# Stationary tiles that begin at 64 modulo 128 bytes, in a two-layer decoder trunk on one core

## The chip, the cores and the metric

The kernel runs on one NeuronCore of a Trainium2 chip. The metric is the device time of one execution in microseconds (us); the kernel before has a median of 2036.69 us over 3 runs (2036.59 to 2038.44). The engines are named as the profile names them: PE is TensorE's matmul, PEld its loading of stationary operands, DVE is VectorE, ACT is ScalarE, POOL is GpSimd, SP is SyncE, which here issues the DMAs. Durations of one instruction are in nanoseconds (ns). A difference of 0.2% is about 4 us.

## What is computed

A batch of one sequence of 512 tokens, 1024 wide, goes through two layers. Each layer is a macaron: half-step SwiGLU feed-forward, token mixer, half-step SwiGLU feed-forward, each with a root-mean-square norm before and after.

```python
for layer in range(2):
    hf = silu(n @ w_gate) * (n @ w_up) @ w_down         # n = rms_norm(x), 1024 -> 2816 -> 1024
    x = x + 0.5 * rms_norm(hf)
    mix = attention(rms_norm(x)) if layer == 0 else mlstm(rms_norm(x))
    x = x + rms_norm(mix)
    x = x + 0.5 * rms_norm(second_swiglu(rms_norm(x)))
```

The attention of layer 0 has 8 stick-breaking heads and 8 dilated heads of 64 columns; the mLSTM of layer 1 has 8 heads of 128 columns. Input and output are float32.

## The kernel before

**Operands.** Every float32 operand of a large product is split into two tiles of the type float32r, `hi` (a rounded copy, made by ACT) and `lo` (the rest, made by DVE or POOL), 4 bytes an element each. A product is three matmuls, hi by hi, hi by lo and lo by hi (`mm3`), which PE adds up in PSUM. Each matmul has its own load of a 128x128 stationary tile, and then lets a moving tile of 128 to 512 columns pass; most have 512. In the profile a matmul's tiles read `out<-moving,stationary`: `pg<-xnh,whi` moves the activations `xnh` over the stationary weights `whi`.

**Stages.** Six phases follow each other: `f00`, `att`, `f01` (layer 0), `f10`, `mls`, `f11` (layer 1). A feed-forward phase (`ffn`) makes gate and up products, `pg<-xnh,whi`, 512 columns at a time, except for the first six chunks, which go by halves of 256 columns; the activation `h` (`glu`); and the down product, partly by a seven-product scheme (`products`, tiles `pc<-dhi,hhi`), partly directly (`po<-dhi,hhi`). There the down weights `dhi`, `dlo` move and the activations `hhi`, `hlo` are stationary. The mixers make projections (`pq`, `ob`), values (`pv<-whi,xnh`, 256 columns, where the weights move and the activations are stationary), heads (`z`, `pv<-p5hi,...`), and an output product (`po<-whi,mhi`, weights moving).

**Order.** The kernel writes the order of work out by itself: `tick` and `spawn` place the elementwise work between matmuls by a modelled clock that counts 0.417 ns a column, and `W` holds delays that were set in that clock. Weights come by DMA from SP through three `raw` buffers, are split by ACT and by DVE or POOL (`chunk`), and wait in four buffers each of `whi` and `wlo`.

**Where tiles lie.** Tiles come from pools, one after another along a partition. The helper `few` widens tiles of a few columns to 128 bytes. In the built program every matmul's moving tile and every stationary tile begins at a multiple of 128 bytes. PE loads the stationary tile of the next matmul while the moving tile of the current one passes, so two reads run side by side. The distance between these two starts (next stationary less current moving) is a multiple of 256 bytes for 6455 of the matmuls with 512 columns of float32r, and 128 more than a multiple for 524. Of these 524, the output products of the mixers (`po<-whi,mhi` and its two partners) are the largest part. With 256 columns it is a multiple of 256 for 1804, and 128 more for 431, the latter mostly in the first chunks of `f01` and `f11`.

Of the kernel before, what the change touches and what calls it, by code (L numbers as in the profile page):

```python
# [11 lines left out]
F32R = mybir.dt.float32r  # L12
# [4 lines left out]
P = 128  # L17
T = 512
D = 1024
KT = 8  # L20
TB = 4
# [21 lines left out]
class Trunk:  # L43
# [73 lines left out]
    def few(self, pool, n, name, bufs=1, dt=F32, rows=P):  # L117

        return pool.tile([rows, 32 if dt is F32 else 64], dt, tag=name, bufs=bufs, name=name)[:, :n]

    def bank(self, name):
        return self.ps.tile([P, 512], F32, tag="ps", name=name)

    def chunk(self, src, n=1024, pool=None, tag="w", bufs=4, eng=None):

        nc, pool = self.nc, pool or self.pp
        raw = self.pp.tile([P, 1024], F32, tag="raw", bufs=3, name="raw")
        nc.sync.dma_start(raw[:, :n], src)
        hi = pool.tile([P, 1024], F32R, tag=tag + "hi", bufs=bufs, name="whi")
        lo = pool.tile([P, 1024], F32R, tag=tag + "lo", bufs=bufs, name="wlo")  # L130
        nc.scalar.copy(hi[:, :n], raw[:, :n])  # L131
        sub = (eng or nc.vector).tensor_sub(lo[:, :n], raw[:, :n], hi[:, :n])  # L132
        if eng:
            self.tc.keep_in_program_order(sub)
        return hi, lo

    def gates(self, src):

        raw = self.pp.tile([P, 1024], F32, tag="raw", bufs=3, name="raw")
        self.nc.sync.dma_start(raw[:, :512], src)  # L140
        w = self.pp.tile([P, 1024], F32R, tag="whi", bufs=4, name="wg")
        v, s = w.rearrange("p (k s m) -> p k s m", k=KT, s=2), raw[:, :512].rearrange("p (k m) -> p k m", k=KT)
        self.nc.scalar.copy(v[:, :, 0, :], s)
        self.nc.vector.tensor_sub(v[:, :, 1, :], s, v[:, :, 0, :])
        return w
# [256 lines left out]

    def hop(self, src):

        hi, lo = [self.fp.tile([P, 256], F32R, tag=t, bufs=12, name=t) for t in ("hhi", "hlo")]
        self.split(hi, lo, src)
        return hi, lo

# [141 lines left out]
    def attention_heads(self, ap, mp, dp):  # L550
            nc, a = self.nc, self.a
            self.exp_ln()
            qk, vs, mix, gone = {}, {}, {}, set()
            done = {i: 0 for i in range(8)}
            cols = [(i, 4 + i) if i < 4 else (8 + i, 12 + i) for i in ORD]
            tri = ap.tile([P, 2, P], F32R, name="tri")
            trif = ap.tile([P, 2, P], F32, tag="f5", bufs=2, name="trif")
            nc.sync.dma_start(trif, a["tri"])
            nc.vector.tensor_copy(tri, trif)
            self.tri = tri  # L560
            self.spawn(self.toeplitz_rows(dp))
            cs = self.first()
            bs = [self.bank("pq") for _ in cs]
            for t in range(2):
                self.half(t)
                for b, c in zip(bs, cs):
                    self.proj(b, c, t * 256, t * 256 + 256)
            for i in range(2):
                self.later(W["qs"], qk, i, self.qk_split(*bs[2 * i:2 * i + 2]))
            scored = {i: 0 for i in range(8)}  # L570

            def lane(r):
                for n, i in enumerate(ORD):
                    while n not in qk:
                        yield 300
                    sl = slice(r * 64, r * 64 + 64)
                    core = self.stick(*qk[n], r) if i < 4 else self.dilated(*qk[n], r, 2 * (i - 4) + r)
                    wait = next(core)
                    scored[n] += 1
                    yield wait  # L580
                    hi, lo = yield from core
                    while i // 2 not in vs:
                        yield 300
                    pv = self.attend2(hi, lo, vs[i // 2][:, :, 2 * (i % 2) + r])
                    m = ap.tile([P, T], F32, tag="m", bufs=1, name="m")
                    nc.scalar.copy(m[sl, :], pv[64:, :])
                    nc.vector.tensor_add(m[sl, :], pv[:64, :], m[sl, :])
                    if n == 7:
                        done[10 + r] = 1
                    while n >= 4 and n - 4 not in gone:  # L590
                        yield 300
                    if n not in mix:
                        mix[n] = [mp.tile([P, T], F32R, tag=t, bufs=4, name=t) for t in ("mhi", "mlo")]
                    mh, ml = mix[n]
                    self.split(mh[sl, :], ml[sl, :], m[sl, :])
                    done[n] += 1
                yield W["end"]
                done[8 + r] = 1

            self.spawn(lane(0))  # L600
            self.spawn(lane(1), W["lane"])

            called = []

            def pair(n):
                self.require(lambda: n < 2 or scored[n - 2] == 2)
                bs = []
                for t in cols[n]:
                    b = self.bank("pq")
                    self.proj(b, self.chunk(a["attn_in"][t]))  # L610
                    bs.append(b)
                self.later(W["qs"], qk, n, self.qk_split(*bs))

            def value(n):
                called.append(n)
                if len(called) > 2:
                    users = [k for k, i in enumerate(ORD) if i // 2 == called[-3]]
                    self.require(lambda: all(done[k] == 2 for k in users))
                self.later(W["avs"], vs, n, self.values(a["attn_v"], n, True))

            def out(k):
                self.require(lambda: done[k] == 2 and done[k + 1] == 2)
                ws = [self.chunk(a["attn_out"][ORD[j]]) for j in (k, k + 1)]
                self.down([mix[j] for j in (k, k + 1)], ws, k == 0)
                gone.update((k, k + 1))

            for w in ATT:
                {"v": value, "p": pair, "o": out}[w[0]](int(w[1]))
            return self.out_first([a["attn_out"][i] for i in ORD[4:]], mix, done)

    def qk_split(self, pq, pk):

        nc, ap = self.nc, self.ap
        ks, qq, ql = [ap.tile([P, 2, T], F32R, tag=t, bufs=2, name=t) for t in ("ks", "qq", "ql")]
        for r in range(2):
            own, oth = slice(64 * r, 64 * r + 64), slice(64 - 64 * r, 128 - 64 * r)
            nc.scalar.copy(ks[own, r, :], pk[own, :])
            nc.scalar.activation(qq[own, r, :], pq[own, :], AF.Copy, scale=0.125)  # L640
            nc.vector.tensor_sub(ks[oth, r, :], pk[own, :], ks[own, r, :])
            nc.vector.scalar_tensor_tensor(ql[own, r, :], pq[own, :], 0.125, qq[own, r, :],  # L642
                                           op0=ALU.mult, op1=ALU.subtract)
            nc.scalar.copy(qq[oth, r, :], qq[own, r, :].bitcast(F32))
            nc.scalar.copy(ql[oth, r, :], ql[own, r, :].bitcast(F32))
        return ks, qq, ql

    def values(self, src, n, stack=False):

        ap = self.ap  # L650
        bs = [self.bank("pv") for _ in range(2)]
        for c in range(2):
            w = self.chunk(src[n, c])
# [5 lines left out]
                    o = bs[tb // 2][:, (tb % 2) * 256:(tb % 2) * 256 + 256]  # L659
                    self.mm3(o, lhs, rhs, k == 0 and tb % 2 == 0, k == KT - 1)  # L660
        if stack:
            vt = ap.tile([P, TB, 4, 2, 64], F32R, tag="vt", bufs=2, name="vt")
            for n in range(2):
                self.split(vt[:, 2 * n:2 * n + 2, :, 0, :], vt[:, 2 * n:2 * n + 2, :, 1, :],
                           bs[n].rearrange("p (t h c) -> p t h c", t=2, h=4))
            return vt
        hi = ap.tile([P, TB, 256], F32R, tag="vhi", bufs=2, name="vhi")
        lo = ap.tile([P, TB, 256], F32R, tag="vlo", bufs=2, name="vlo")
        for n in range(2):
            self.split(hi[:, 2 * n:2 * n + 2, :], lo[:, 2 * n:2 * n + 2, :],  # L670
                       bs[n].rearrange("p (t c) -> p t c", t=2))
# [155 lines left out]
    def mlstm_heads(self, ap, mp, dp):  # L827
# [4 lines left out]
            nc.sync.dma_start(hg, a["head_g"])  # L832
            onf = ap.tile([P, P], F32, tag="n2", bufs=1, name="onf")
            nc.gpsimd.memset(onf, 1.0 / P)
            ones, onr = [ap.tile([P, P], F32R, name=n) for n in ("ones", "onr")]
            nc.vector.tensor_scalar(ones, onf, float(P), None, op0=ALU.mult)
            nc.vector.tensor_copy(onr, onf)
            cs = self.first()
# [117 lines left out]
    def conv(self, bq, bk, h):  # L956
# [11 lines left out]
            nc.scalar.activation(c, c, AF.Silu)  # L968
        self.exp_ln()
        for n, c, sc in (("q", cs[0], P ** -0.5), ("k", cs[1], 1.0)):  # L970
            hi = ap.tile([P, T], F32R, tag=n + "hi", bufs=2, name=n + "hi")
            lo = ap.tile([P, T], F32R, tag=n + "lo", bufs=2, name=n + "lo")
            nc.scalar.activation(hi, c, AF.Copy, scale=sc)
            nc.vector.scalar_tensor_tensor(lo, c, sc, hi, op0=ALU.mult, op1=ALU.subtract)
            out.append((hi, lo))
# [169 lines left out]
```

## Time and profile before

| | |
|---|---|
| median of 3 runs | 2036.69 us |
| the profiled execution's own time | 2036.48 us |
| its span, first to last instruction | 2034.8 us |
| PE busy | 1971.4 us (97%), 9876 matmuls |
| PEld busy | 1668.0 us (82%) |
| DVE, ACT, POOL busy | 1319.9 us (65%), 955.9 us (47%), 503.3 us (25%) |
| DMA | 200.51 MB, mean 99 GB/s |
| mean granted clock of TensorE | 0.990 |

The span is the time between the first and the last instruction; 1.7 us of the execution lie around it. Busy shares are unions over the span. A matmul's duration in the profile contains the time in which it is already in the pipeline behind the one before, so the duration (389 ns for 512 columns) is not what one costs: that is read from the distance between starts, in the timeline or in a piece of the chain of waits that holds a known count of matmuls.

### The profile page before, as it was taken

Reading aid. Unit: us, or ns where it says so; the run is one execution under the profiler, and the core shown is the slowest. Engines: PE = TensorE matmul, PEld = TensorE weight load, DVE = VectorE, ACT = ScalarE, POOL = GpSimd, SP = SyncE. Lnnn points to the kernel's source line nnn. Section 1 sums busy time; section 2 is a strip of 40 time slices with the busy share of each in tenths; the row PEclk is TensorE's granted clock in tenths of the full one; section 3 lists DMA queues with packets and bytes.
Section 4 is the critical chain, followed back from the end, with each engine's and each line's share of the span. In section 5 each row is a group of like instructions: output and inputs, shape, how many; then the busy total and the mean of one; then the engine's idle time right before and its main releaser. Section 6 shows DMA issues by size and latency. Waiting matters only on the chain.

```text
span 2034.8 us, 25965 instructions
## 1 busy us (share of the span) xinstructions
PE 1971.4 (97%) x9876; PEld 1668.0 (82%) x9876; DVE 1319.9 (65%) x2016; ACT 955.9 (47%) x1649; POOL 503.3 (25%) x374
## 2 busy tenths in 40 slices
PE   8999999999997999999999999999999989999998
PEld 7888888888886978888788888888889868888887
DVE  6766654666678676665487666547776786676643
ACT  5443333477786353333244333325877654433321
POOL 4322312101004343221343232121010143332111
PEclk9999999999998999999999999999999989999999
DMA  5333332232122233333124333321433222423321
GB/s 186 125 95 107 100 114 75 84 117 71 54 73 83 86 125 100 104 107 112 56 79 135 107 99 101 109 71 51 155 104 117 91 96 83 132 94 109 108 83 42
DMA packets 56119, 200.51 MB, mean 99 GB/s; under 512 B 6521, under 2 KB 6649, under 8 KB 55994
## 3 DMA queue, kind: packets, MB, share of 16 engines
q1 hardware_dynamic: 55992, 198.85, 30.2%
q8 instruction: 77, 1.26, 0.3%
q14 instruction: 48, 0.39, 0.1%
q10 hardware_dynamic: 2, 0.00, 0.0%
HBM read 196.65 MB, written 4.80 MB: 99 GB/s over the span
## 4 chain that ended last, share of the span: by engine, by line
PE 72%; DVE 8%; issue 8%; ACT 6%; POOL 4%; DMA 1%; SPq 0%; POOLq 0%; DVEq 0%; ACTq 0%
PE pg L72 40%; PE pc L72 14%; PE pq L72 5%; PE po L72 4%; PE pv L72 4%; PE ob L72 2%; DVE x L289 2%; PE z L72 1%; POOL r L222 1%; DVE dlo L188 1%; DVE xa L259 1%; POOL yg L283 1%; DVE xnl L188 1%; POOL wlo L132 1%; POOL h L399 1%
## 5 line engine op out<-in xcount | busy, mean ns | idle before, releaser
L72 PE MATMUL pg<-xnl,whi 128*128 128x512 f32 (+1 forms) x1568 | 576.5, 368 | 6.0 <-DVE xnl L188 6.0
L72 PE MATMUL pg<-xnh,whi 128*128 128x512 f32 (+1 forms) x1568 | 577.0, 368 | 0.1
L72 PE MATMUL pg<-xnh,wlo 128*128 128x512 f32 (+1 forms) x1568 | 576.5, 368 | 0.0
L131 ACT CAST whi<-raw 128x1024 fp32r<-128x1024 f32 x248 | 259.7, 1051 | 436.5 <-issue 189.6
L132 DVE TENSOR_TENSOR wlo<-raw,whi 128x1024 fp32r<-128x1024 f32 x227 | 291.1, 1284 | 185.6 <-ACT whi L131 180.6
L72 PEld LDWEIGHTS pg<-xnl,whi 128*128 128x128 f32 x1568 | 295.7, 189 | 55.6 <-DVE xnl L188 6.7
L72 PEld LDWEIGHTS pg<-xnh,whi 128*128 128x128 f32 x1568 | 295.4, 188 | 49.2 <-ACT xnh L187 0.5
L72 PEld LDWEIGHTS pg<-xnh,wlo 128*128 128x128 f32 x1568 | 295.4, 188 | 48.8
L399 POOL TENSOR_TENSOR h<-h,rs 128x512 f32<-128x512 f32 x88 | 142.7, 1621 | 762.1 <-ACT h L398 733.9
L188 DVE TENSOR_TENSOR dlo<-raw,dhi 128x512 fp32r<-128x512 f32 x240 | 188.8, 807 | 89.2 <-ACT dhi L187 88.8
L187 ACT CAST dhi<-raw 128x512 fp32r<-128x512 f32 x240 | 146.6, 621 | 195.4 <-DMA raw<-down 150.7
L400 DVE TENSOR_TENSOR h<-h,pg 128x512 f32<-128x512 f32 x88 | 60.1, 683 | 217.5 <-PE pg L72 214.3
L72 PE MATMUL pc<-dhi,hhi 128*128 128x512 f32 x448 | 176.1, 393 | 4.6 <-ACT hhi L187 4.6
L72 PE MATMUL pc<-dhi,hlo 128*128 128x512 f32 x448 | 176.0, 393 | 0.0
L72 PE MATMUL pc<-dlo,hhi 128*128 128x512 f32 x448 | 175.2, 391 | 0.0
L484 DVE TENSOR_TENSOR y<-y,pc 128x512 f32<-128x512 f32 x192 | 128.9, 678 | 5.6 <-PE pc L72 5.4
L72 PE MATMUL pq<-xnh,whi 128*128 128x512 f32 (+1 forms) x312 | 110.2, 354 | 0.7 <-DVE ql L642 0.7
L72 PE MATMUL pq<-xnl,whi 128*128 128x512 f32 (+1 forms) x312 | 109.7, 352 | 0.3 <-DVE xnl L188 0.3
L72 PE MATMUL pq<-xnh,wlo 128*128 128x512 f32 (+1 forms) x312 | 109.6, 352 | 0.0
L188 DVE TENSOR_TENSOR hlo<-h,hhi 128x256 fp32r<-128x256 f32 x208 | 103.3, 515 | 8.0 <-ACT hhi L187 7.8
L187 ACT CAST hhi<-h 128x256 fp32r<-128x256 f32 x208 | 78.9, 405 | 57.5 <-DVE h L400 51.0
L72 PEld LDWEIGHTS pc<-dhi,hhi 128*128 128x128 f32 x448 | 84.9, 189 | 22.8 <-ACT hhi L187 5.5
(237 smaller groups left out, 3319.7 us busy)
## 6 DMA issues: line engine op xcount, KB each, us to landing
raw<-gate SPq DMA_DIRECT2D x88, 512.0 KB, 3.5
raw<-up SPq DMA_DIRECT2D x88, 512.0 KB, 3.4
raw<-down SPq DMA_DIRECT2D x88, 512.0 KB, 3.4
raw<-mlstm_in SPq DMA_DIRECT2D x24, 512.0 KB, 3.5
raw<-attn_in SPq DMA_DIRECT2D x16, 512.0 KB, 3.4
bt<-rows SPq DMA_DIRECT2D x8, 896.0 KB, 4.2
gb<-norm_g SPq DMA_DIRECT2D x11, 512.0 KB, 3.9
raw<-attn_v SPq DMA_DIRECT2D x8, 512.0 KB
```

The costliest lines, as they stand in the source:

```text
L72: self.nc.tensor.matmul(out, lhsT=lhsT, rhs=rhs, start=start, stop=stop, skip_group_check=True)
L131: nc.scalar.copy(hi[:, :n], raw[:, :n])
L132: sub = (eng or nc.vector).tensor_sub(lo[:, :n], raw[:, :n], hi[:, :n])
L187: self.nc.scalar.copy(hi, src)
L188: self.nc.vector.tensor_sub(lo, src, hi)
L222: nc.gpsimd.tensor_tensor(r, v, self.mhalf, op=ALU.pow)
L259: nc.vector.scalar_tensor_tensor(xs[h], xt[:, sl], r, g[h], op0=ALU.mult, op1=ALU.mult)
L283: nc.gpsimd.tensor_mul(yg[0], yt[:, :512], g[:, :512])
L289: nc.vector.scalar_tensor_tensor(dst, yg[h], r, xt[:, sl], op0=ALU.mult, op1=ALU.add)
L399: self.nc.gpsimd.tensor_mul(h, h, self.rs)
L400: self.nc.vector.tensor_mul(h, h, pu)
L484: self.nc.vector.tensor_add(dst, dst, b)
```

## The change

A new helper `odd` takes a tile that is 32 elements (128 bytes) wider and gives back the part that begins 16 elements (64 bytes) in. It is used for the weights that are stationary in the projections (`whi`, `wlo`, `wg`), the activations of the down product (`hhi`, `hlo`), the keys (`ks`, `khi`, `klo`), the values (`vt`, `vhi`, `vlo`) and the constants `tri`, `ones`, `onr`.

```diff
+    def odd(self, pool, n, name, tag=None, bufs=1, dt=F32R):
+        return pool.tile([P, n + 32], dt, tag=tag or name, bufs=bufs, name=name)[:, 16:16 + n]
...
-        hi = pool.tile([P, 1024], F32R, tag=tag + "hi", bufs=bufs, name="whi")
-        lo = pool.tile([P, 1024], F32R, tag=tag + "lo", bufs=bufs, name="wlo")
+        hi = self.odd(pool, 1024, "whi", tag + "hi", bufs)
+        lo = self.odd(pool, 1024, "wlo", tag + "lo", bufs)
...
-        hi, lo = [self.fp.tile([P, 256], F32R, tag=t, bufs=12, name=t) for t in ("hhi", "hlo")]
+        hi, lo = [self.odd(self.fp, 256, t, bufs=12) for t in ("hhi", "hlo")]
...
-        ks, qq, ql = [ap.tile([P, 2, T], F32R, tag=t, bufs=2, name=t) for t in ("ks", "qq", "ql")]
+        ks = self.odd(ap, 2 * T, "ks", bufs=2).rearrange("p (r t) -> p r t", r=2)
+        qq, ql = [ap.tile([P, 2, T], F32R, tag=t, bufs=2, name=t) for t in ("qq", "ql")]
...
-            hi = ap.tile([P, T], F32R, tag=n + "hi", bufs=2, name=n + "hi")
-            lo = ap.tile([P, T], F32R, tag=n + "lo", bufs=2, name=n + "lo")
+            hi, lo = [self.odd(ap, T, n + s, bufs=2) if n == "k" else
+                      ap.tile([P, T], F32R, tag=n + s, bufs=2, name=n + s) for s in ("hi", "lo")]
```

The other uses (`wg`, `tri`, `vt`, `vhi`, `vlo`, `ones`, `onr`) are of the same form. In the built program each float32r matmul now has one operand at 64 modulo 128 bytes and the other at a multiple of 128. Where `whi` and `wlo` are the moving side (values and output products, 1152 matmuls) and where `ks` is (64), it is the moving tile that begins at 64. The distance between the next stationary tile and the current moving one is 64 modulo 256 for 3411 and 192 modulo 256 for 3537 of the matmuls with 512 columns; with 256 columns, 1133 and 1079. Buffers of `whi` are now 4224 bytes apart instead of 4096, so both distances occur in turn.

The order of instructions on PE, DVE, ACT, POOL and SP is the same in both built programs, row by row; PE's and DVE's waits are too. On ACT, POOL and SP about a dozen instructions at the borders of pools wait for another set of semaphores, because buffers of other tiles lie there now.

## Rows read from the trace of the kernel before

**Rows 1.** The page: busy us, share of the span, instructions.

```profile
PE 1971.4 (97%) x9876; PEld 1668.0 (82%) x9876; DVE 1319.9 (65%) x2016; ACT 955.9 (47%) x1649; POOL 503.3 (25%) x374
```

**Rows 2.** Stretches: us from:to, length, busy us (instructions) by engine, PEclk, DMA share, GB/s.

```profile
100.00:200.00 100.00, 100.00 (x443) 82.75 (x442) 63.21 (x98) 40.32 (x70) 29.24 (x18) 1.00 0.31 98
400.00:500.00 100.00, 94.87 (x613) 85.58 (x612) 65.15 (x101) 79.07 (x126) 10.31 (x16) 1.00 0.30 99
500.00:600.00 100.00, 97.92 (x570) 85.68 (x569) 65.95 (x122) 79.28 (x136) 8.31 (x16) 1.00 0.23 75
600.00:700.00 100.00, 87.40 (x551) 76.10 (x550) 76.50 (x140) 50.30 (x103) 30.47 (x22) 0.95 0.22 74
1020.00:1022.90 2.90, 2.90 (x8) 2.28 (x7) 2.05 (x4) 1.02 (x3) 0.55 (x1) 0.50 0.00 0
```

**Rows 3.** Chain of waits in order of time: start us, us, what.

```profile
105.72 27.21 PE pg L72 x120
...
1562.00 11.51 PE pv L72 x96
```

**Rows 4.** Timeline of PE: start us, us, engine, line, op, tiles, form, count.

```profile
1504.33 0.64 PE L72 MATMUL po<-whi,mhi 128*128 128x512 f32 x2
...
1510.84 0.64 PE L72 MATMUL po<-whi,mlo 128*128 128x512 f32 x2
```

**Rows 5.** Timeline of PE, 256 columns at the start of `f01`.

```profile
659.65 0.28 PE L72 MATMUL pg<-xnh,whi 128*128 128x256 f32 x1
...
662.02 0.28 PE L72 MATMUL pg<-xnh,wlo 128*128 128x256 f32 x1
```

**Rows 6.** Timeline of PE at the lower clock.

```profile
1019.96 0.63 PE L72 MATMUL po<-dhi,hhi 128*128 128x512 f32 x1
...
1022.52 0.60 PE L72 MATMUL po<-dhi,hhi 128*128 128x512 f32 x1
```

**Rows 7.** Timeline of PE, gate weights: stationary tiles of 128 and 64 columns in turn.

```profile
1399.31 0.28 PE L72 MATMUL pq<-xnl,wg 128*64 128x256 f32 x1
...
1400.48 0.28 PE L72 MATMUL pq<-xnl,wg 128*64 128x256 f32 x1
```

**Rows 8.** Groups by form: line, engine, op, tiles, form, count, busy us, mean ns, idle before.

```profile
L72 PE MATMUL pg<-xnh,whi 128*128 128x512 f32 x1248 | 485.8, 389 | 0.0
L72 PE MATMUL pc<-dhi,hhi 128*128 128x512 f32 x448 | 176.1, 393 | 4.6 <-ACT hhi L187 4.6
L72 PE MATMUL pg<-xnh,whi 128*128 128x256 f32 x320 | 91.2, 286 | 0.1
L72 PE MATMUL pq<-xnh,whi 128*128 128x512 f32 x200 | 78.4, 392 | 0.7 <-DVE ql L642 0.7
L72 PE MATMUL po<-dhi,hhi 128*128 128x512 f32 x192 | 76.4, 398 | 1.0 <-ACT hhi L187 1.0
L72 PE MATMUL pv<-whi,xnh 128*128 128x256 f32 x256 | 72.6, 284 | 1.0 <-DVE m L587 0.8 <-DVE ks L641 0.2
L72 PE MATMUL po<-whi,mhi 128*128 128x512 f32 x128 | 46.8, 407 | 0.1
L72 PE MATMUL pq<-xnh,whi 128*128 128x256 f32 x112 | 31.8, 287 | 0.0
L72 PE MATMUL ob<-xnh,whi 128*128 128x512 f32 x64 | 25.0, 390 | 0.0
```

**Rows 9.** Groups by form, DVE: the convolution's shifted columns beside an unshifted tile.

```profile
L964 DVE SCALAR_TENSOR_TENSOR cv<-pq,cw,cv 128x511 f32<-128x511 f32 x16 | 11.9, 744 | 6.1 <-ACT cv L962 6.1
L964 DVE SCALAR_TENSOR_TENSOR cv<-pq,cw,cv 128x509 f32<-128x509 f32 x16 | 11.9, 742 | 0.1
L974 DVE SCALAR_TENSOR_TENSOR klo<-cv,khi 128x512 fp32r<-128x512 f32 x8 | 5.9, 739 | 7.7 <-ACT khi L973 7.7
```

**Rows 10.** Waits of PE: for whom, us in total, times, longest.

```profile
PE pt L264 <- DVE xa L259: 20.4, 12, 7.4
PE pt L264 <- DVE y L259: 6.2, 2, 3.2
PE pg L72 <- DVE xnl L188: 6.0, 3, 2.9
```

More of the change, by code (lines that the diff above doesn't have):

```diff
@@ L140, in gates @@
         self.nc.sync.dma_start(raw[:, :512], src)
-        w = self.pp.tile([P, 1024], F32R, tag="whi", bufs=4, name="wg")
+        w = self.odd(self.pp, 1024, "wg", "whi", 4)
         v, s = w.rearrange("p (k s m) -> p k s m", k=KT, s=2), raw[:, :512].rearrange("p (k m) -> p k m", k=KT)
@@ L555, in attention_heads @@
             cols = [(i, 4 + i) if i < 4 else (8 + i, 12 + i) for i in ORD]
-            tri = ap.tile([P, 2, P], F32R, name="tri")
+            tri = self.odd(ap, 2 * P, "tri").rearrange("p (a k) -> p a k", a=2)
             trif = ap.tile([P, 2, P], F32, tag="f5", bufs=2, name="trif")
@@ L661, in values @@
         if stack:
-            vt = ap.tile([P, TB, 4, 2, 64], F32R, tag="vt", bufs=2, name="vt")
+            vt = self.odd(ap, TB * 512, "vt", bufs=2).rearrange("p (b h s c) -> p b h s c", b=TB, h=4, s=2)
             for n in range(2):
@@ L666, in values @@
             return vt
-        hi = ap.tile([P, TB, 256], F32R, tag="vhi", bufs=2, name="vhi")
-        lo = ap.tile([P, TB, 256], F32R, tag="vlo", bufs=2, name="vlo")
+        hi, lo = [self.odd(ap, TB * 256, t, bufs=2).rearrange("p (b c) -> p b c", b=TB) for t in ("vhi", "vlo")]
         for n in range(2):
@@ L834, in mlstm_heads @@
             nc.gpsimd.memset(onf, 1.0 / P)
-            ones, onr = [ap.tile([P, P], F32R, name=n) for n in ("ones", "onr")]
+            ones, onr = [self.odd(ap, P, n) for n in ("ones", "onr")]
             nc.vector.tensor_scalar(ones, onf, float(P), None, op0=ALU.mult)
```

## The prediction

> **What bounds the kernel now.** I read the busy shares first: PE is busy 97% of the span, and no other engine is over 65% [rows 1]. The stretches show where that holds without a gap: between 100 and 200 us, in a feed-forward phase, PE is busy 100.00 of 100 us and the others 63 or less [rows 2]. In the mixers it is less plain: from 400 to 600 us PE is busy 94.87 and 97.92, and ACT 79 [rows 2]. The waits of PE for other engines are short: the largest is 20.4 us in 12 times, at the transposes between phases [rows 10]. So a change in what one matmul costs goes nearly whole into the time in the feed-forward phases, and in part in the mixers.
>
> What one matmul costs is the distance between starts. A piece of the chain with 120 gate and up matmuls of 512 columns takes 27.21 us, 226.75 ns each; a piece with 96 value matmuls of 256 columns takes 11.51 us, 119.9 ns each [rows 3]. At the lower of TensorE's two levels, 1.2 GHz (PEclk 0.50 from 1020.00 to 1022.90 us [rows 2], after PE had stood idle at a border of phases), six matmuls of 512 columns take 1022.52 - 1019.96 = 2.56 us, 426.7 ns each [rows 6], which is 512 columns at 1.2 GHz with nothing beside. Half of it, 213.3 ns, is what 512 columns need at 2.4 GHz; 256 need 106.7. So at the full clock each matmul spends 13.4 ns (512) or 13.2 ns (256) more than its columns, and at the half clock none, though a stationary tile is loaded for each in both. That looks like two reads in each other's way when they run fast. Three more rows say that it is. With stationary tiles of 64 and 128 columns in turn, ten matmuls of 256 columns take 1400.48 - 1399.31 = 1.17 us, 117.0 ns, an excess of 10.3 instead of 13.2 [rows 7]: less to load, less excess. The output products of the mixers, whose stationary tile lies 128 bytes (modulo 256) off the moving one, take 1510.84 - 1504.33 = 6.51 us for 28 matmuls, 232.5 ns [rows 4], 5.8 ns more than the others. And at the start of `f01`, where the same distance occurs with 256 columns, 20 matmuls take 2.37 us, 118.5 ns [rows 5], 1.4 ns less. So the excess depends on the addresses, which is all that this change touches.
>
> **The change part by part.** It removes no instruction, adds none and moves none. What changes is the distance of the two reads: from 0 (or 128) to 64 and 192 modulo 256, about half of the matmuls each. No row shows either distance, so the cost of one matmul is bounded by the nearest rows: at best the excess is gone (213.3 and 106.7 ns, as at the half clock), at worst of what is seen on an average it is 232.5 ns for 512 and 119.9 for 256. Between these ends, the values seen move by some 6 ns when the distance moves by 128; I take one such step, down: half of the excess, 6.7 ns, goes.
>
> The counts, each group three times for the three products [rows 8]: in the feed-forward phases 3 x (1248 + 448 + 192) = 5664 matmuls of 512 columns and 3 x 320 = 960 of 256; in the mixers 3 x (200 + 64 + 128) = 1176 of 512, of which 384 are the output products at 232.5, and 3 x (256 + 112) = 1104 of 256.
>
> Feed-forward: 5664 x 6.7 = 37.9 us, 960 x 6.7 = 6.4, together 44.3 us, all on the path, as between 100 and 200 us [rows 2]. Mixers: 1176 x 6.7 = 7.9, 384 x 5.8 = 2.2 for the output products that come down to the others, 1104 x 6.7 = 7.4, together 17.5; since ACT is nearly as busy as PE there and lanes of heads wait for it, I count half, 8.7. The smaller groups (scores, constants) I leave out. Sum 53.0 us.
>
> Some is given back. At the borders of the phases the norm of a row block runs on DVE, ACT and POOL under the cover of matmuls; when these get 3% faster (6.7 of 226.7), the cover shrinks and the wait that follows grows by as much. PE's waits at these places are the 20.4, 6.2 and 6.0 us of [rows 10]; with some twenty row blocks at covers of about 8 us (my estimate from the stretch 600 to 700 us, where PE is idle 12.6 us [rows 2]) that is 20 x 8 x 0.03 = 5 us. Net 48 us.
>
> The writers of the moved tiles are ACT, DVE and POOL. I cost their part at nothing: the convolution writes and reads at 4 and 12 bytes past a tile's start and takes 744 and 742 ns, against 739 ns for an unshifted tile of the same size [rows 9]. If a start at 64 did cost them 1%, that is 13 us of DVE's 1319.9 and 10 of ACT's 955.9, under PE's cover in the feed-forward phases, and 3 to 4 us in the mixers. The waits that now name other semaphores at borders of pools are about a dozen; those on SP have the next gains and first weights queued behind them, which three `raw` buffers cover. I price them at 0, between -2 and +3 us.
>
> The profiled execution has 2036.48 us (span 2034.8 and 1.7 around it), 0.2 us under the median, so the sums are good for the median as they are: 2036.5 - 48 = 1988 us.
>
> The Trainium skill has a rule against this change: SBUF — State Buffer, "Who interferes with whom", says that PE has two independent read ports, one for the moving operand and one for loading weights, and that PE and ACT never wait on anyone. By it the distance of two tiles could not matter and the sum would be 0. The trace does not agree in full: 226.75, 232.5, and 426.7 = 2 x 213.3 for the same work [rows 3, 4, 6]. And TensorE: Matmul & The Clock Gate, "Back-to-back issue gap", gives a floor of about 2.5 ns a matmul at the full clock; by it 10.9 of the 13.4 ns could go at most.
>
> **The rivals.**
> First, the two reads no longer meet at all. For it: at the half clock the excess is 0 [rows 6], so nothing but their meeting need be in it. Against: the shortest average seen at full speed with a whole stationary tile is 118.5 for 256 columns [rows 5], an excess of 11.8. Price: 5664 x 13.4 + 960 x 13.2 = 88.6 us, mixers (1176 x 13.4 + 384 x 5.8 + 1104 x 13.2) / 2 = 16.3, given back 20 x 8 x 0.06 = 10: 95 us, 1942 us.
>
> Second, on the other side: the new distance is a bad one. The mechanism: in one matmul the moving read goes through 2048 bytes and the loading read through 512, so they do not keep their distance; a distance of 0 lets both begin together and part, while any other lets them meet later, for longer. For it: the only other distance in the trace is worse for 512 columns, 232.5 against 226.75 [rows 3, 4]. Against: with 256 columns it is not, 118.5 against 119.9 [rows 3, 5]. It decides from an average of 227.4 ns on (0.65 ns over 6840 matmuls is the 4 us of 0.2%). At 232.5 for all: 5664 x 5.8 = 32.9, less 960 x 1.4 = 1.3, mixers 792 x 5.8 / 2 = 2.3: +34 us, 2070 us. If only one of the two distances is bad, 17 us: 2054 us.
>
> Third, nothing changes: the excess is a matter of how much is loaded [rows 7], not of where, and the 5.8 ns at the output products come from what else differs there (weights move, pairs share a stationary tile). Then 2036.5 us, at most 384 x 5.8 = 2 us less. Against it: the 118.5 of the projections [rows 5], which are otherwise like the 119.9.
> The Trainium skill's rule on PE's two read ports (SBUF — State Buffer, "Who interferes with whom") comes out here.
>
> **How the numbers follow.** Half of the excess goes, or a part about it: 0.40, with its own range of 1965 to 2028. All of it goes: 0.18. Nothing changes: 0.12. Worse: 0.30. Faster by over 0.2% (about what a measurement of this kernel can tell from no change) is the first two, 0.58; same 0.12; slower 0.30. The range reaches from 1940, the end of the first rival, over no change to 2060, which leaves out the worse half of the second, some 0.13, and a little below.
>
> **What would show it.** Right: a piece of the chain with 120 matmuls `pg` of 512 columns takes 26.4 us (220 ns each), one with 96 `pv` about 10.9; PE stays at 95% or more, and its waits for the transposes grow by 3 to 8 us. First rival: 25.6 us. Second: 27.5 or more, or two spacings in turn, one for each distance. Third: 27.2. The forecast is wrong in its mechanism if the matmuls get closer and the time does not follow, that is if PE's waits take more than a third of the gain; and the writers' step is wrong if the casts and subtractions into moved tiles change their mean by over 1%.

## The result: about 1% slower

The kernel after has a median of 2058.85 us (2058.01 to 2060.7, 4 runs) against 2037.57 (2036.59 to 2039.59, 4 runs) for the kernel before: a ratio of 1.0104, 95% interval 1.0087 to 1.0122. The forecast was 1988 us with a range up to 2060, so the range holds the time and the direction is wrong. The profiled execution of after has a span of 2057.7 us, 22.9 more than before, and the profile explains that one.

The page of after, busy time by engine, answers to [rows 1]:

```profile
PE 1994.3 (97%) x9876; PEld 1665.7 (81%) x9876; DVE 1319.3 (64%) x2016; ACT 955.5 (46%) x1649; POOL 504.4 (25%) x374
```

PE has grown by 22.9 us, with the same 9876 instructions; no other engine has changed by more than 2.3 us. Everything added is PE's own time.

The feed-forward stretch of [rows 2] (the columns are PE, PEld, DVE, ACT, POOL, then the granted clock):

```profile
100.00:200.00 100.00, 100.00 (x434) 81.25 (x433) 60.33 (x94) 37.42 (x65) 28.14 (x18) 1.00 0.30 100
```

Here PE was and is busy all the time at the full clock, and gets through 434 matmuls instead of 443: they became dearer. The later stretches of [rows 2] cannot be compared in this way, as the kernel after lies some 6 us behind there and does other work in them.

The chain of waits tells which ones became dearer (start, us, what; to set beside [rows 3]):

```profile
1127.17 27.89 PE pg L72 x120
...
1374.31 5.72 DVE x L294 x2
...
1481.64 11.06 PE pq L72 x48
...
1521.54 6.85 PE po L72 x30
...
1579.18 11.27 PE pv L72 x96
...
1699.73 10.42 PE pg L72 x90
```

120 matmuls of 512 columns take 27.89 us, 232.4 ns each instead of 226.75. 96 of 256 columns take 11.27, 117.4 instead of 119.9; the 90 of 256 columns at the start of `f11` take 10.42, 115.8 ns. The output products, which the change takes from a distance of 128 to 64 or 192, take 6.85 us for 30, 228.3 ns against the 232.5 of [rows 4]. Over the whole timelines, at the full clock and where PE had no gap, 512 columns went from 227.4 to 231.6 ns and 256 columns from 119.5 to 116.1. That is 6904 x 4.2 = +29 us and 2146 x 3.4 = -7 us, +22 together, as much as the span grew. By distance, 512 columns take 232.8 ns at 64 and 230.4 at 192. The loss can also be followed place by place, beside these rows of the chain before:

```profile
1356.82 5.67 DVE x L289 x2
...
1465.14 10.90 PE pq L72 x48
...
1682.27 10.73 PE pg L72 x90
```

The row at 1374.31 stands at 1356.82 in the profile before, the one at 1481.64 at 1465.14. The four phases up to the end of `f10` lose 17.5 us, the first half of `mls` gives 1.0 back, and from 1699.73, in `f11` (1682.27 before), to the end another 5.4 us are lost.

The writers of the moved tiles did not change (line, engine, operation, form, count, then busy us and mean ns of one; answers to [rows 9]):

```profile
L979 DVE SCALAR_TENSOR_TENSOR klo<-cv,khi 128x512 fp32r<-128x512 f32 x8 | 5.9, 733 | 7.7 <-ACT khi L978 7.7
L137 DVE TENSOR_TENSOR wlo<-raw,whi 128x1024 fp32r<-128x1024 f32 x227 | 289.3, 1276 | 196.2 <-ACT whi L136 190.8 <-PE nb L72 1.1
```

`klo` takes 733 ns against 739, `wlo` 1276 against 1284 before. PE's waits for other engines, as in [rows 10], hardly moved either:

```profile
PE pt L269 <- DVE xa L264: 18.7, 7, 7.5
PE pg L72 <- DVE xnl L193: 6.3, 3, 3.0
```

### The profile page after: what moved, and what is told of

It reads as the page before. It is cut to its first block, busy times and chain, and to the rows that moved or that the text cites. A ratio compares the mean times of both kernels' runs of the same rounds, so it can differ in the third digit from the quotient of the medians.

```text
span 2057.7 us, 25967 instructions
## 1 busy us (share of the span) xinstructions
PE 1994.3 (97%) x9876; PEld 1665.7 (81%) x9876; DVE 1319.3 (64%) x2016; ACT 955.5 (46%) x1649; POOL 504.4 (25%) x374
## 5 line engine op out<-in xcount | busy, mean ns | idle before, releaser
L72 PE MATMUL pg<-xnl,whi 128*128 128x512 f32 (+1 forms) x1568 | 584.0, 372 | 6.3 <-DVE xnl L193 6.3
L72 PE MATMUL pg<-xnh,wlo 128*128 128x512 f32 (+1 forms) x1568 | 584.5, 373 | 0.0
L72 PE MATMUL pg<-xnh,whi 128*128 128x512 f32 (+1 forms) x1568 | 583.8, 373 | 0.1
L137 DVE TENSOR_TENSOR wlo<-raw,whi 128x1024 fp32r<-128x1024 f32 x227 | 289.3, 1276 | 196.2 <-ACT whi L136 190.8
```

The costliest lines, as they stand in the source:

```text
L72: self.nc.tensor.matmul(out, lhsT=lhsT, rhs=rhs, start=start, stop=stop, skip_group_check=True)
```

## Experiments

Four theories are named in the expectations. A: two reads of PE meet, and only the distance of their starts counts. B: the place of the stationary tile itself counts. C: the moving read alone is slow, because it does not keep pace with 4-byte elements at 2.4 GHz. D: PSUM or the change of the stationary tile costs it. Distances below are starts of the stationary less the moving tile, in bytes modulo 256. Two runs are kernels with PE alone, a row of equal matmuls per case, and each was executed once; the others are the whole kernel with tiles placed otherwise.

**e1: the spacing by distance, PE alone.** The loop that is run for each case (columns that move, columns that are loaded, first byte of each):

```diff
+                nc.tensor.matmul(o[:m, :n], lhsT=sta[:, s:s + m], rhs=mov[:, mo // 4:mo // 4 + n],
+                                 start=i == 0, stop=i == reps - 1, skip_group_check=True)
```

> This kernel leaves out the whole computation: it is PE alone, 40 equal matmuls of float32r in a row for each of 79 cases, with chosen first bytes of the moving and the stationary tile (modulo 1024), moved columns n and loaded columns l. Theory A (two reads meet, and only the distance of their starts counts): n512 at distance 0 takes 226.7 ns, at 64 about 233, at 128 about 232.4, at 192 about 230.4; n256 119.9, 116, 118.6, 116; moving 64 and stationary 64 is like distance 0, moving 64 and stationary 128 like distance 64; fewer loaded columns give less excess, at 8 loaded columns under 2 ns. Theory B (the place of the stationary tile itself counts): moving 64 and stationary 64 is like distance 64 (233), moving 64 and stationary 0 or 128 is 226.7 for 512 columns. Theory C (the moving read alone is slowed, by a share of its columns): 8 loaded columns give the same excess as 128, about 18 ns for 512 columns and 9 for 256, at every distance but 0.

The timeline of PE (start, us of the row of 40, then the case: `n` columns moving, `d` the distance, `m..s..` the two places themselves, `l` columns loaded):

```profile
21.88 9.23 PE L113 MATMUL n512d0c<-mov,sta 128*128 128x512 f32 x40
...
58.68 9.49 PE L113 MATMUL n512d64c<-mov,sta 128*128 128x512 f32 x40
...
133.18 9.34 PE L113 MATMUL n512d192c<-mov,sta 128*128 128x512 f32 x40
...
225.49 4.95 PE L113 MATMUL n256d0c<-mov,sta 128*128 128x256 f32 x40
...
244.46 4.70 PE L113 MATMUL n256d64c<-mov,sta 128*128 128x256 f32 x40
...
329.50 9.24 PE L113 MATMUL n512m64s64c<-mov,sta 128*128 128x512 f32 x40
338.58 9.49 PE L113 MATMUL n512m64s128c<-mov,sta 128*128 128x512 f32 x40
...
380.09 4.87 PE L113 MATMUL n256m64s128c<-mov,sta 128*128 128x256 f32 x40
...
487.40 4.71 PE L113 MATMUL n256l64d0c<-mov,sta 128*64 128x256 f32 x40
...
524.08 9.41 PE L113 MATMUL n512l8d0c<-mov,sta 128*8 128x512 f32 x40
533.33 9.43 PE L113 MATMUL n512l8d64c<-mov,sta 128*8 128x512 f32 x40
```

A row holds 39 spacings and one matmul's own 0.39 us (0.28 for 256 columns): (9.23 - 0.39) / 39 = 226.7 ns. The means of the last 24 spacings of each row:

| distance | 0 | 64 | 128 | 192 |
|---|---|---|---|---|
| 512 columns, ns | 226.67 | 233.33 | 233.33 | 228.88 |
| 256 columns, ns | 120.00 | 113.33 | 120.00 | 117.79 |

This is the result in small: both new distances are worse than 0 with 512 columns and better with 256. For 512 columns, both tiles at 64 cost what both at 0 do (226.67), and moving at 64 with stationary at 128 costs what 0 with 64 does (233.33): the place itself does not count, and B falls. 256, 320 and 448 repeat 0, 64 and 192. With 256 columns this is less clean: moving at 64 with stationary at 128 took 117.79 ns, not 113.33, and a distance of 320 took 117.75 (e8 comes back to this). A's distance holds, but its other half does not: with 8 columns loaded instead of 128, 512 columns still take 231.1 and 231.7 ns at the distances 0 and 64, and 256 columns 116.67 at both. There is next to nothing to meet, and the excess stays, as C said, though C had excepted the distance 0. What does go with the small load is the difference between the two distances, 0.6 ns instead of 6.67.

**e2: every stationary tile at distance 0** (the edit is against the kernel after; `few`, the helper for narrow tiles, pads to 256 bytes too):

```diff
-        return pool.tile([P, n + 32], dt, ...)[:, 16:16 + n]
+        return pool.tile([P, n + 64], dt, ...)[:, 0:0 + n]
```

> All of the kernel, with every stationary and every moving tile at the same place modulo 256, so distance 0 for all 6979 matmuls of 512 columns and all 2235 of 256 (before: 524 and 431 were at 128). Theory A: the 524 fall from 232.4 to 226.8 ns, 2.9 us, the 431 rise from 118.6 to 119.8, 0.5 us: 2 us less than before, 0.9988 to 0.9995. Theory B: as before, 1.000. Theory C: as A.

2036.7 us against 2038.01, 0.9994 (0.9985 to 1.0004). The loss is gone, with the new helper, its names and wider tiles still there. The interval holds what A and what B expected, so this run does not tell them apart. In its chain:

```profile
1115.85 27.20 PE pg L72 x120
...
1426.06 6.37 DMA bt<-rows
1465.28 10.90 PE pq L72 x48
...
1561.83 11.51 PE pv L72 x96
...
1681.76 10.79 PE pg L72 x90
```

27.20 us are 226.67 ns each, 11.51 are 119.9: the bare rows' spacings at 0 are the kernel's.

**e3: nearly every one at 64** (as e2, with another slice):

```diff
+        return pool.tile([P, n + 64], dt, ...)[:, 16:16 + n]
```

> All of the kernel, with the changed kernel's odd tiles, but padded so that the distance is 64 modulo 256 for 6576 of the 6979 matmuls of 512 columns (where the weights move it is 192), in place of 64 and 192 in turn. Theory A: 512 columns at 232.9 instead of a mean of 231.6 and 256 columns at 115 to 117: about 8 us more than the changed kernel, 1.013 to 1.016 of before. Theory B: the same as the changed kernel, 1.010. Theory C, in which what spoils it is that the distance changes from one matmul to the next: less than the changed kernel, 1.000 to 1.006.

2072.17 us, 1.0164 (1.0149 to 1.0179). 28.00 us for 120 are 233.3 ns, 11.30 for 96 are 117.7, where the value weights move and so have the distance 192. Twice as many matmuls at 64 as in after cost half as much again, and without the turn of two distances, so it is not the turn that costs.

```profile
1132.85 28.00 PE pg L72 x120
...
1590.20 11.30 PE pv L72 x96
```

**e4: what the excess is made of, PE alone.** Elements of 2 bytes (`bf`), a moving tile of which every second element is read (`two`), the same 128 columns read four times (`wrap`), fine steps of distance, 32 partitions (`rows`), two PSUM banks in turn (`banks`), and matmuls that do not add up (`each`):

```diff
+                if how == "bf":
+                    s = so[i % len(so)] // 2
+                    lhs, rhs = stab[:, s:s + m], movb[:, mo // 2:mo // 2 + n]
+                elif how == "two":
+                    rhs = mov[:, mo // 4:mo // 4 + 2 * n].rearrange("p (c t) -> p c t", t=2)[:, :, 0]
```

> This kernel leaves out the whole computation: PE alone, 30 equal matmuls in a row per case. The first cases go through the distances 0 to 252 in steps of 4 bytes, for 512 and 256 columns; the others change one thing at distance 0, 64 and 128: bf are bfloat16 operands (2 bytes an element), two is a moving read of every second element, wrap a moving read of the same 128 columns four times (64 columns for n256), rows uses 32 partitions, banks two PSUM banks in turn, each does not add up in PSUM. Theory C (the moving read of 4-byte elements by itself falls behind at 2.4 GHz): bf has an excess under 4 ns (216 ns for 512 columns) at every distance and with 8 loaded columns too, two has more excess than the plain read, rows, banks and each have the same as the plain read, 227 at distance 0 and 233 at 64. Theory D (PSUM or the change of the stationary tile costs it): bf has the same 227 and 233, and banks or each differ from the plain read. Of the fine distances theory C expects one or two multiples of 4 bytes that repeat exactly and are shorter than their neighbours, and none under 220 for 512 columns.

```profile
188.27 6.97 PE L203 MATMUL n512d120c<-mov,sta 128*128 128x512 f32 x30
...
250.64 7.28 PE L203 MATMUL n512d164c<-mov,sta 128*128 128x512 f32 x30
...
580.95 6.64 PE L203 MATMUL n512l128d128bf<-movb,stab 128*128 128x512 bf16 x30
587.52 6.64 PE L203 MATMUL n512l8d0bf<-movb,stab 128*8 128x512 bf16 x30
...
626.88 13.79 PE L203 MATMUL n512l128d0two<-mov,sta 128*128 128x512 f32 x30
640.49 13.78 PE L203 MATMUL n512l128d64two<-mov,sta 128*128 128x512 f32 x30
...
709.05 6.96 PE L203 MATMUL n512l8d0wrap<-mov,sta 128*8 128x512 f32 x30
...
845.80 7.16 PE L203 MATMUL n512l128d64each<-mov,sta 128*128 128x512 f32 x30
```

With 2-byte elements 512 columns take 215.83 ns at all three distances tried (0, 64, 128) and with 8 columns loaded as with 128, for the same PSUM writes. With 4-byte elements, matmuls that do not add up leave 512 columns at 226.8 (distance 0) and 233.33 (64), and two banks in turn give 233.33 at 64 as well. So D falls as far as PSUM goes. A 2-byte stationary tile is also loaded in a shorter time (98 ns a load against 188 in the trace), but 8 loaded columns of 4 bytes have as short a load (88 ns) and keep the excess, so it is not the load either. With every second element read, 512 columns take 453.7 ns (640.49 - 626.88 over 30), twice 226.67, for the same columns and products: what counts is the bytes that the moving read passes. Four passes over the same 128 columns take 226.67 too (8 loaded, distance 0). So the excess at the best distance is the moving read's own pace, as C has it. 226.67 / 213.33, 113.33 / 106.67 and 453.33 / 426.67 are all 17/16: 2048 bytes of a partition in 226.67 ns, 9.0 bytes a ns. Over 4-byte steps of distance 512 columns took 226.67 to 237.6 ns and 256 columns 113.33 to 122.2, never less. So 17/16 is a floor in these rows, and the distance decides what comes on top. At 0, 512 columns stand on the floor and 256 are 6.67 ns above; at 64 it is the other way round. The 32-partition rows fell to the lower clock and say nothing on this.

**e5: 64 for 256 columns only, 0 for 512.** If the sign goes by width, each width can have its distance:

```diff
+# where tiles begin, in elements past a multiple of 256 bytes
+O512, O256, OVAL = 0, 16, 48
...
-        return pool.tile([P, n + 32], dt, ...)[:, 16:16 + n]
+        return pool.tile([P, n + 64], dt, ...)[:, off:off + n]
...
-            w = self.chunk(src[n, c])
+            w = self.chunk(src[n, c], off=OVAL)
```

`O256` is passed for the first chunks of every phase and the gate weights, `OVAL` for the values, whose weights move.

> All of the kernel, every tile at the same place modulo 256 as in the run at distance 0, but with distance 64 for 2069 of the 2235 matmuls of 256 columns (first chunks of each phase, gate weights, values); the 512 columns stay at distance 0. If width decides the sign: 1330 matmuls fall from 119.8 to 115.1 (6 us), 768 of the values to 116.5 (2.5 us): 0.9940 to 0.9975 of before, and faster than both kernels. If the width is not what decides, but the phase in which they run: 1.000 to 1.005.

2033.45 us against 2037.32, 0.9979 (0.997 to 0.9989): faster than both kernels.

```profile
1112.82 27.20 PE pg L74 x120
...
1422.87 6.78 DMA bt<-rows
...
1463.95 10.90 PE pq L74 x48
...
1560.28 11.31 PE pv L74 x96
...
1679.81 10.22 PE pg L74 x90
```

512 columns are as in e2, and the 90 of 256 take 113.6 ns instead of 119.9. Over the whole timelines the 256-column spacings fall from 119.8 to 115.1 ns, some 10 us over 2146, but the span is only 3.0 us shorter. Part of where it goes can be seen in the first half of `mls`: at the row `bt<-rows` e5 leads e2 by 1426.06 - 1422.87 = 3.19 us, at the next row shown by 1465.28 - 1463.95 = 1.33. Between them lies this wait of PE, in e2 and in e5, and the 27 matmuls behind it (timeline, then stretches, with the granted clock behind the five engines):

```profile
1450.15 0.50 PE L72 MATMUL z<-qhi,khi 128*128 128x512 f32 x1 [0.55 <-ACT khi L978]
1447.27 0.50 PE L74 MATMUL z<-qhi,khi 128*128 128x512 f32 x1 [2.09 <-ACT khi L980]
```

```profile
1450.15:1454.98 4.83, 4.83 (x27) 4.14 (x28) 4.62 (x7) 1.96 (x4) 0.00 (x0) 1.00 0.48 147
1447.27:1453.64 6.37, 6.37 (x27) 5.52 (x28) 4.62 (x7) 2.28 (x4) 0.00 (x0) 0.73 0.55 187
```

PE comes sooner to the tile `khi` than ACT has it ready and stands idle for 2.09 us instead of 0.55. After that the granted clock is 0.73 on the mean, with a part of the stretch at the lower level, and the same 27 matmuls take 6.37 us instead of 4.83. A gain of PE in a mixer can thus cost more than the wait alone. The expectation (0.9940 to 0.9975) had the sign and too large a size.

**e6: the reverse, 64 for 512 columns only** (`O512, O256, OVAL = 16, 0, 0`, otherwise e5).

> All of the kernel, the reverse: distance 64 for 6573 of the matmuls of 512 columns (and for those of the heads), 0 for 2076 of 256 columns. If width decides: 6979 x 6 ns = 42 us in the span at most, of which the mixers keep half: 1.017 to 1.022, more than the 1.0164 with both at 64. If the 256 columns do not count: 1.0164.

2072.88 us, 1.0171 (1.0155 to 1.0186), with 233.3 ns and 119.8 ns in its chain. e5 and e6 differ in nothing but which width has which distance, and come out on opposite sides. e3, which has 64 for nearly all, lies beside e6 within the noise, so what the 256 columns save there does not show in the time.

```profile
1135.00 28.00 PE pg L74 x120
...
1589.78 11.50 PE pv L74 x96
```

**e7: every one at 192** (`[:, 48:48 + n]` in e3).

> All of the kernel, with odd tiles 192 bytes past a multiple of 256: distance 192 for 6576 of the matmuls of 512 columns (weights moving: 64), in place of 64 and 192 in turn. If each matmul costs what the bare rows of its distance cost (512 columns 228.9 ns at 192 against 226.7 at 0 and 233.3 at 64; 256 columns 117.8 against 120.0 and 113.3): 6979 x 2.2 = 15 us, less about 1 us that the 256 columns keep: 1.005 to 1.008 of before. If the turn of the two distances or another thing in the changed kernel made its 192 cost 230.4: 1.010 to 1.013.

2047.11 us against 2038.5, 1.0045 (1.0032 to 1.0059). 27.47 us for 120 are 228.9 ns, the bare rows' 228.88. So the second of the new distances costs too: a third of what the first does by the spacing (2.2 of 6.67 ns), and 1.0045 is just under the range expected.

```profile
1120.03 27.47 PE pg L72 x120
...
1568.77 10.90 PE pv L72 x96
```

**e8: every one at 16** (`[:, 4:4 + n]`), which in e1 cost 226.67 ns, as 0 does.

> All of the kernel, with odd tiles 16 bytes past a multiple of 256 (weights moving: distance 240). The bare rows have 226.67 ns for 512 columns at 16, the same as at 0, and 118.3 for 256. If the bare rows hold and 226.67 is a floor that any good distance reaches: 0.998 to 1.000 of before. If only a start at the same multiple of 64 or 256 is good in the kernel, where tiles and lengths change from one matmul to the next: 1.005 or more.

2068.26 us (2056.68 to 2072.61), 1.0152 (1.013 to 1.0175). The bare rows failed here (0.998 to 1.000 was expected if they hold), and the chain of the quickest run shows how:

```profile
168.95 27.20 PE pg L72 x120
...
1118.02 28.00 PE pg L72 x120
```

The same stream at the same distance runs at 226.67 ns in an earlier phase and at 233.33 in a later one: two repeating patterns. At 0 (e2) the 512 columns kept to the quick one, 227.0 ns on the mean of the whole timeline. With 256 columns there are two patterns too. The 96 value matmuls lie at the same places modulo 256, 64 apart, in e5 and in e7, and take 11.31 us in one, 117.8 ns each, and 10.90 in the other, 113.5. In e4 the row `each` took 117.75 ns at 64 where the plain row took 113.33. So the odd rows of e1 with 256 columns need no effect of the place. What sets the pattern was not found.

## Why the prediction was wrong

**The step that failed** is the reading of the excess: "That looks like two reads in each other's way when they run fast", and from it "half of the excess, 6.7 ns, goes". Of the 13.4 ns at 512 columns, all is the pace of the moving read with 4-byte elements, and none goes when less is loaded; 226.67 is the floor (e1, e4), so there was nothing to win, and another distance could at best be as good. The lower bound of 213.3 ns was out of reach. Each row fits this reading as well, or better:
- [rows 6], the half clock without excess, was taken to show that the excess comes from a meeting. It needs 2048 bytes in 426.7 ns, 4.8 a ns, where the read can give 9.0.
- [rows 7], 117.0 ns with loads of 64 and 128 columns in turn, was taken as "less to load, less excess". In e1 256 columns at distance 0 take 113.33 with 64 loaded and 120.00 with 128, mean 116.67; but 116.67 with 8 loaded, and 512 columns at distance 0 get slower, 231.1, with 8. The width of the load changes what comes on top of the floor, in either direction, and the floor stays.
- [rows 4], 232.5 at distance 128, was the one warning for 512 columns, and e1 has 233.33 for it. I had it as an argument of the second rival.

**The sizes.** The 256 columns did gain, 3.4 ns instead of 6.7, and the output products came down by 4.2 instead of 5.8 + 6.7. The 512 columns, forecast at -6.7, went +4.2. With e1's numbers at half of each distance the term is 6904 x (6.67 + 2.21) / 2 = +31 us, and 2146 x (6.67 + 2.21) / 2 = -10 for the others, against +29 and -7 in the trace.

**The second rival** was what happened, in place and sign. Its end for "only one of the two distances is bad", 2054, is close to 2058.85, though both are bad, by 6.7 and 2.2 ns. Its mechanism, two reads that start together and part or else meet later and longer, is not shown and not excluded. It fails in that 512 columns at distance 0 get slower when only 8 are loaded (231.1); for it stands that the difference between the distances 0 and 64 is 6.67 ns with 128 loaded and 0.6 with 8. The marks that it set, 27.5 us or more and two spacings, are in the trace: 27.89, with 232.8 and 230.4 by distance. That the range holds the time is owed to this rival, for half of which it was drawn up to 2060, and not to the forecast's own mechanism. The first rival (no meeting, 1942) could not be. The third falls with e2, e3 and e7, which differ in places alone.

**What held.** What comes on top of the floor depends on addresses; what PE lost went whole into the time (22.9 us busy, 22.9 us of span), while of the 10 us that it saved in e5 only about 3 did; the writers cost nothing; the waits at borders of pools cost nothing that shows, as e2, whose tiles lie elsewhere too, is within 0.2% of before.

The Trainium skill, TensorE: Matmul & The Clock Gate, "Back-to-back issue gap", gives N / 2.4 + 2.5 ns as the gap of a single matmul of N columns at the full clock, that is 2.5 ns over the columns' time. e4 agrees for 2-byte elements, 215.83 - 213.33 = 2.5, and not for 4-byte ones, whose floor with 512 columns is 13.3 above. SBUF — State Buffer, "Who interferes with whom", also of the Trainium skill, has PE wait on no one. That 8 loaded columns leave the excess in place agrees with it; that the distance to the load changes it by 6.67 ns does not, and how PE's two reads come to that stays open.

## What to carry to other kernels

Before excess spacing is put down to a conflict, measure the same matmul with 2-byte elements, with every second element read, and with next to nothing loaded: here these told the pace of one read from two reads meeting. The half clock did not, as both readings give no excess there. With float32r operands, keep stationary and moving tiles at the same place modulo 256 bytes for 512 columns, and try 64 for 256 columns, each width by itself (e5: 0.2% of the time). A spacing measured in a bare stream must be seen in the kernel too, as e8 shows.

## What the runs showed of the hardware that was not expected

At the full clock, moving tiles of 4-byte elements have a floor of 17/16 of the columns' time (226.67, 113.33 ns) in e1 and e4. On top come up to 11 ns by the distance of the two starts, with opposite sign for 512 and 256 columns at 64; for 512 columns the values repeat after 256 bytes. At one distance the same stream can have two steady spacings: 226.67 and 233.33 ns at 16 (512 columns), 113.33 and 117.8 at 64 (256 columns).

Matmuls over 32 partitions, back to back, ran at the lower clock in the one run that has them. The stretches of e4 (PE, PEld, DVE, POOL, then the granted clock) and the timeline:

```profile
700.00:750.00 50.00, 50.00 (x303) 33.12 (x302) 0.00 (x0) 0.00 (x0) 1.00 0.00 1
750.00:800.00 50.00, 50.00 (x166) 41.70 (x164) 0.00 (x0) 0.00 (x0) 0.55 0.00 0
```

```profile
760.46 13.00 PE L203 MATMUL n512l128d64rows<-mov,sta 32*128 32x512 f32 x30
```

PE was busy without a gap in both stretches. In the second, where 32 of 128 rows are used, the clock fell to the lower level, 1.2 GHz (0.55 over the stretch), and 512 columns took 426.7 ns (773.26 - 760.46 over 30). From 810 to 815 us, with 128 rows again, it was 1.00.
